# Decoder layer on one core: raw weights of the first projection set loaded a pair ahead into tiles of their own, and their decode products moved to the pair's end

## The chip, the cores and the metric

The kernel runs on one core of a Trainium2 chip. A core has an engine for matrix products (PE, with its weight loads shown apart as PEld), three engines for elementwise work (DVE, ACT, POOL) and a queue engine (SP) that here issues nearly all transfers between the chip's large memory (DRAM below) and the core's own memory. The metric is the device time of one execution in microseconds (us): the median of three runs before the change is 1027.93 us.

## The reference

One layer of a decoder, for a prompt of 2048 tokens and for 8 single tokens of a running decode with their own states. Everything is in fp32.

```
h = rmsnorm(x, norm_g)
p = h @ w_in                                   # 1024 -> 8 groups of 512
rq, rk, rv, rg, hq, hf, hi, hgate = split(p, 8)
rq, rk = rotary(rq, pos), rotary(rk, pos) * RET_DK ** -0.5
o_ret = chunked_decay_recurrence(rq, rk, rv, log_gamma, s_ret)     # 4 heads, fixed decay
o_ret = head_rmsnorm(o_ret, ret_g) * silu(rg)
logf  = logaddexp(log(lb), log1p(-lb) + log_sigmoid(hf))
kin   = (1 - lb) * sigmoid(-hf)
o_hg  = chunked_decay_recurrence(silu(hq), kin, hi, logf, s_hg)    # 4 heads, decay per channel
o_hg  = head_rmsnorm(o_hg, hg_g) * silu(hgate)
y = rmsnorm(x + concat(o_ret, o_hg) @ w_out, final_norm_g)
```

The recurrence keeps a state per head, S_t = diag(f_t) S_(t-1) + k_t v_t^T with o_t = S_t^T q_t, and is evaluated in chunks. Outputs are y for the prompt and for the decode tokens, and the new states of both.

## The kernel before, in words

**Products.** An fp32 operand is split into a high and a low part; a product is three matmuls, high x high, low x high and high x low (`three`, L350). The prompt is worked in *pairs*: 256 tokens at a time against 1024 columns of weights, both cut into 2 x 2 blocks, so that a pair takes seven block products instead of eight. A block product is 4 x 3 matmuls of 128 x 512, so a pair is 84 matmuls. The seven need sums of the weight blocks (operands T1 to T4 beside the raw B12, B22 and `wv`, which stands for B11 and B21) and sums of the token blocks (S1 to S4, made in `tok_ops`; `ab_h`, `ab_l` are the parts of the raw token blocks, L117 and L118).

**Stages.** There are three sets of eight pairs. Set 0 (pairs 0 to 7) makes the values, set 1 (pairs 8 to 15) the queries and gate of the retention, set 2 (pairs 16 to 23) its keys and the gate of the other branch, and beside set 2 the retention runs chunk by chunk (`r_steps`). Then come the projections and level products of the HGRN2 heads, and the output projection, in pairs again. Pairs 0 and 1 are done plainly, with eight block products each, while the weights arrive.

**Decode tokens.** The 8 tokens are carried through the same weights as a small extra product: `four` (L590) multiplies their 8 columns with the raw weights, 4 products of 256 columns for each 128 rows of weights. For the values this is `decode_values` (tile pvd) in pair 0; for sets 1 and 2 it is `wg_decode` (tile pgd).

**How the weights of the next set come in.** During set 0, in pairs 2 to 5, the raw weights of set 1 are brought in for k = 0 to 3: `wg_load(1, k)` loads rows k and k + 4 (tiles wgr1k, 512 KB each, L517), `wg_decode` multiplies them with the decode tokens, and `wg_spool` makes the four sums in place on DVE (`w_sums`, L503 to L506) and stores them in DRAM (ws1T1 to ws1T4, L529). In pair 7 they are fetched again. Set 2 goes the same way during set 1. The raw tiles come from a pool `rawp` with few buffers, which the token loads `xr`, the sums S and others share. The tiles of pool `vq` have one buffer for each tag (zh0, zl0, zh1, zl1, rk, rg and others), used by different things at different times.

**What sets the order.** PE's instructions keep the order in which they are written. The other engines' are ordered by a list scheduler, except that `behind(f)` ties what f issues on DVE, ACT and SP behind the last instruction issued on each. The pair loop (L908) fills a table `after`: what stands at key n is issued behind block product n (0 to 6) of the pair, and n - 0.5 is the middle of product n. Each of PE's small insertions between block products is placed in this way: the decode products, `spread` (transposes of the token statistics, tile prs, L288, from `rs_all`, which POOL makes out of `stats_sum`, ACT, L269), and `r_flip` (transposes of a chunk's keys, tile pkt, L726, whose input rk DVE makes in the rotary step at L375). The copy of prs, rb (L290), is what the scaled token blocks of the next pair need (L302), and from them come ab_h and ab_l.

**At the start.** Behind pair 0's products stand two bursts of `decode_values`, four weights in each. The sums of the value weights (`wv_comb`: `w_sums`, then the split into T1 to T4) are made in place on the raw tiles wvr0 to wvr7, so a sum waits until the decode products of its weights have read them. Before all of it stand small warm-up matmuls (L86).

**Later places.** `hgrn_rec` gives each step of a head a position within its unit, and `MOVE` shifts some of them; `levels2(1)` is a group of small products (tile plh). In the output projection the table `wd_at` places the decode steps: `d_ms` and `d_rs` normalise (DVE, tile do, L1392), `d_tr` transposes on PE (tile pdt, L1396), `wd_mm` multiplies from pair 4 on.

Of the kernel before, what the change touches and what calls it, by code (L numbers as in the profile page):

```python
# [10 lines left out]
F32 = mybir.dt.float32  # L11
# [3 lines left out]
ALU = mybir.AluOpType  # L15
# [26 lines left out]
def step_kernel(ctx, tc, a, out):  # L42
# [40 lines left out]
    for n in range(14):  # L83
        pe.matmul(wu, ones, ones, start=True, stop=True)
    for n in range(12):
        pe.matmul(wu[:32, :16], ones[:, :32], ones[:, :16], start=True, stop=True)  # L86
# [415 lines left out]
    def w_sums(r0, r1):  # L502
        dve.tensor_tensor(r0[:, 0], r0[:, 1], r0[:, 0], op=ALU.subtract)  # L503
        dve.tensor_tensor(r0[:, 1], r1[:, 1], r0[:, 1], op=ALU.subtract)
        dve.tensor_tensor(r1[:, 1], r1[:, 1], r0[:, 0], op=ALU.subtract)
        dve.tensor_tensor(r1[:, 0], r1[:, 0], r1[:, 1], op=ALU.subtract)  # L506
        return ("T2", r1[:, 1]), ("T3", r0[:, 1]), ("T1", r0[:, 0]), ("T4", r1[:, 0])

# [5 lines left out]
    def wg_load(n, k):  # L514
        for kk in (k, k + 4):
            wr[kk] = rawp.tile([P, 2, GW], F32, tag="raw", name=f"wgr{n}{kk}")
            sp.dma_start(wr[kk].rearrange("p g n -> p (g n)"), a[f"w_{n}"][kk])  # L517

    pgd = {}

    def wg_decode(n, k):
        if n not in pgd:
            pgd[n] = ps_o.tile([P, 256], F32, tag="o", name=f"pgd{n}")
        for kk in (k, k + 4):
            four(pgd[n], xs[:, kk], wr[kk].rearrange("p a b -> p (a b)"), kk == 0, kk == KT - 1)

# [60 lines left out]
    def four(ps, x, w, first, last):  # L587

        for j in range(4):
            pe.matmul(ps[32 * j : 32 * j + x.shape[1]], x, w[:, j * 256 : j * 256 + 256], start=first, stop=last)  # L590

# [203 lines left out]
    def r_steps(p):  # L795
# [112 lines left out]
    for i in range(2, n_tok):  # L908
# [267 lines left out]

    MOVE = {(0, 0, 1): 0.065, (0, 1, 3): 0.065, (0, 2, 1): 0.065, (1, 0, 1): 0.125, (1, 3, 1): 0.11}

# [693 lines left out]
    for n in range(4):  # L1872
# [108 lines left out]
```

## Time and profile before

| | |
|---|---|
| median of three runs | 1027.93 us (1026.58 to 1029.33) |
| the profiled execution | 1030.97 us, of which the span is 1029.1 us |
| granted clock of PE | 0.998 |
| PE busy | 1014.0 us, 99% of the span |
| DVE, ACT, POOL busy | 734.2, 550.3, 122.8 us |
| bytes moved | 255.63 MB, mean 248 GB/s |

The profile is one execution, and times in it count from the start of its span. A row of the timeline gives start and duration in us, the engine, the line, what is written from what, and in brackets how long the engine stood idle before it and what ended that. In a row of PE the duration is longer than the distance to the next matmul, since matmuls overlap; distances from start to start tell what a matmul costs. The view of waits sums such idle time by what was waited for. A row of windows gives, for a stretch of time, the busy time of each engine (with the number of instructions), the granted clock, the share of time in which the 16 DMA engines were busy, and the GB/s moved.

### The profile page before, as it was taken

What the parts mean: (1) busy time and instruction counts of PE and PEld (TensorE: products, weight loads), DVE (VectorE), ACT (ScalarE), POOL (GpSimd) and SP (SyncE); (2) the same over time, 40 slices, a digit from 0 to 9 for tenths busy, and PEclk for the clock granted to TensorE, in tenths of its full rate; (3) what the DMA queues carried; (4) which work ended last, traced back from release to release, by engine and by line L of the source; (5) the groups of instructions that cost most, each with busy time, mean ns of one, the idle gap of its engine ahead of it and who ended that gap; (6) DMA issues with size and microseconds to landing.
All of it is one profiled execution on the core that took longest, in us unless ns stands there. A gap on an engine that the chain in (4) does not pass through costs nothing.

```text
span 1029.1 us, 21541 instructions
## 1 busy us (share of the span) xinstructions
PE 1014.0 (99%) x8366; PEld 841.7 (82%) x8366; DVE 734.2 (71%) x1353; ACT 550.3 (53%) x1211; POOL 122.8 (12%) x231
## 2 busy tenths in 40 slices
PE   9999999999999999999999999999999999999997
PEld 7767778887778888888888899898888878878775
DVE  7887666888675885576666768768768576667886
ACT  7863435735434765555564665667556476433242
POOL 0200001000000101111111100111022112301122
PEclk9999999999999999999999999999999999999999
DMA  8699998878999965567766697555864496565652
GB/s 290 210 327 330 332 334 275 326 263 313 312 326 304 359 238 184 189 226 247 233 222 205 210 334 268 193 185 200 283 216 133 129 362 227 180 252 204 227 186 103
DMA packets 151271, 255.63 MB, mean 248 GB/s; under 512 B 11424, under 2 KB 79280, under 8 KB 151040
## 3 DMA queue, kind: packets, MB, share of 16 engines
q1 hardware_dynamic: 141408, 225.03, 64.7%
q0 software_dynamic: 7440, 24.76, 6.3%
q10 hardware_dynamic: 2320, 4.46, 1.2%
q8 instruction: 66, 1.08, 0.4%
q14 instruction: 37, 0.30, 0.1%
HBM read 166.51 MB, written 87.69 MB: 247 GB/s over the span
## 4 chain that ended last, share of the span: by engine, by line
PE 82%; DMA 4%; DVE 1%; issue 0%; SPq 0%; POOLq 0%; ACT 0%; POOL 0%; DVEq 0%; ACTq 0%
PE po L350 10%; PE pjqh L1032 9%; PE pjfh L1032 8%; PE py L1659 4%; PE plh L1246 2%; PE pur L741 1%; PE par L734 1%; PE puh L1115 1%; PE por L747 1%; PE por L749 1%; PE poh L1131 1%; DMA oT1h<-t_dramh 1%; PE poh L1133 1%; PE pv20a L350 1%; PE pv21a L350 1%; PE pv22a L350 1%
## 5 line engine op out<-in xcount | busy, mean ns | idle before, releaser
L1032 PE MATMUL pjfh<-xh,w_h 128*128 128x512 f32 (+2 forms) x160 | 59.4, 372 | 0.0
L1032 PE MATMUL pjqh<-xh,w_h 128*128 128x512 f32 (+2 forms) x160 | 58.9, 368 | 0.0
L1226 ACT ACTIVATE kepth<-kh 128x1024 f32<-128x1024 f32 x24 | 25.4, 1060 | 62.0 <-DVE kh L1216 62.0
L1032 PE MATMUL pjqh<-xh,w_l 128*128 128x512 f32 (+2 forms) x160 | 55.7, 348 | 0.0
L1032 PE MATMUL pjfh<-xh,w_l 128*128 128x512 f32 (+2 forms) x160 | 55.7, 348 | 0.0
L1032 PE MATMUL pjfh<-xl,w_h 128*128 128x512 f32 (+2 forms) x160 | 55.6, 348 | 0.0
L1032 PE MATMUL pjqh<-xl,w_h 128*128 128x512 f32 (+2 forms) x160 | 55.6, 347 | 0.0
L1216 DVE TENSOR_TENSOR kh<-kh,fph 128x512 f32<-128x512 f32 x48 | 33.4, 696 | 22.8 <-PE plh L1246 19.8
L118 DVE TENSOR_TENSOR ab_l<-xr,ab_h 128x512 fp32r<-128x512 f32 (+1 forms) x40 | 37.5, 954 | 11.6 <-ACT ab_h L117 11.6
L772 DVE SCALAR_TENSOR_TENSOR obr<-por,omr,rg 128x128 f32<-128x128 f32 x64 | 18.0, 344 | 33.3 <-POOL omr L764 28.2
L762 ACT ACTIVATE obr<-por 128x128 f32<-128x128 f32 x64 | 16.8, 277 | 44.4 <-PE por L749 40.6
L117 ACT ACTIVATE ab_h<-xr 128x512 fp32r<-128x512 f32 (+1 forms) x40 | 32.4, 838 | 11.3 <-DVE xr L302 11.3
L1032 PEld LDWEIGHTS pjqh<-xh,w_h 128*128 128x128 f32 x160 | 30.4, 190 | 4.8 <-issue 1.2
L1032 PEld LDWEIGHTS pjfh<-xh,w_h 128*128 128x128 f32 x160 | 30.2, 189 | 4.1 <-issue 0.4
L1032 PEld LDWEIGHTS pjqh<-xh,w_l 128*128 128x128 f32 x160 | 30.1, 188 | 4.1
L1032 PEld LDWEIGHTS pjfh<-xh,w_l 128*128 128x128 f32 x160 | 30.1, 188 | 4.0
L409 ACT ACTIVATE vo<-vo 128x512 f32<-128x512 f32 x32 | 20.1, 629 | 24.7 <-DVE vo L403 10.8
L1219 DVE TENSOR_TENSOR qqh<-qqh,fph 128x512 f32<-128x512 f32 x48 | 32.8, 683 | 0.0
L1032 PEld LDWEIGHTS pjqh<-xl,w_h 128*128 128x128 f32 x160 | 30.2, 189 | 3.0
L1032 PEld LDWEIGHTS pjfh<-xl,w_h 128*128 128x128 f32 x160 | 30.2, 189 | 2.7
L302 DVE SCALAR_TENSOR_TENSOR xr<-xr,g_in,rb 128x256 f32<-128x256 f32 x64 | 27.1, 480 | 7.3 <-DMA xr<-in_x_t 4.2
L1659 PE MATMUL py<-woh,oc_h 128*128 128x512 f32 x64 | 26.6, 415 | 0.0
(1839 smaller groups left out, 3335.0 us busy)
## 6 DMA issues: line engine op xcount, KB each, us to landing
xr<-a_dram SPq DMA_DIRECT2D x24, 512.0 KB
S<-s_dram SPq DMA_DIRECT2D x24, 512.0 KB
xn<-in_x_prompt SPq DMA_DIRECT2D x32, 256.0 KB
xr<-in_x_t SPq DMA_DIRECT2D x16, 512.0 KB
a_dram<-xr SPq DMA_DIRECT2D x16, 512.0 KB
s_dram<-S SPq DMA_DIRECT2D x16, 512.0 KB
wgr<-in_w SPq DMA_DIRECT2D x16, 512.0 KB
xr<-a_dram SPq DMA_DIRECT2D x32, 256.0 KB
```

Of the source, the lines that this page charges most:

```text
L117: act.activation(h, src, AF.Copy)
L118: dve.tensor_tensor(l, src, h.bitcast(F32), op=ALU.subtract)
L302: dve.scalar_tensor_tensor(r[:, k], r[:, k], g_in[:, kk : kk + 1], spread_to[i], op0=ALU.mult, op1=ALU.mult)
L350: pe.matmul(ps, xx, ww, start=(first and n == 0), stop=(last and n == 2), skip_group_check=more)
L409: act.activation(o, src, AF.Silu)
L772: dve.scalar_tensor_tensor(o[:, cc], po[:, h], ms[:, h : h + 1], rb_of[c, "g"][:, cc], op0=ALU.mult, op1=ALU.mult)
L1032: pe.matmul(ps, ww[:, kk], x[:, k, b0 : b0 + n], start=(k == 0 and i == 0), stop=(k == KT - 1 and i == 2),)
L1216: dve.tensor_tensor(kv[:, :, 0, :], kv[:, :, 0, :], two[:, :, 1:2].to_broadcast([P, nb, b]), op=ALU.mult)
L1219: dve.tensor_tensor(qv[:, :, 1, :], qv[:, :, 1, :], two[:, :, 0:1].to_broadcast([P, nb, b]), op=ALU.mult)
L1226: act.activation(ss[:, 512:], k[:, :HALF], AF.Copy)
L1246: pe.matmul(dst[32 * i : 32 * i + 32, c], kk, qq, start=True, stop=True)
L1659: pe.matmul(ps, o[:, kk], w[:, k % 4, i * 512 : (i + 1) * 512], start=(k == 0 and n == 0), stop=(k == KT - 1 and n == 2),)
```

## The change

1. `wg_load` for set 1 takes tiles of its own for six of the eight rows: for even k both rows, as two halves of 256 KB each in the tags zh0, zl0 (row k) and zh1, zl1 (row k + 4) of `vq`; for odd k row k + 4 in rk and rg, while row k stays in `rawp`. `four`, `wg_decode` and `w_sums` take such a list of two halves; the products and the four subtractions are the same.
2. The loads of set 1 are issued, tied behind what stands before them, after product 1 of pair 2 for k = 0, and after product 5 of pairs 2, 3 and 4 for k = 1, 2, 3; before, each was issued after product 0 of the pair that used it (pairs 2 to 5). Its decode products and sums follow product 6, the last of the pair; before they followed product 4 (5 in pair 3).
3. `decode_values` for all eight weights stands in one burst behind pair 0's last products; before, half of it stood behind the second quarter.
4. The statistics of the pair after next (`stats_sum`, `stats_load`) are issued after product 1 in every pair; before, after product 2 in all but pair 2.
5. In the retention's first step `r_flip(0)`, `r_score(0)` and `r_update(0)` are each issued half a product later.
6. `levels2(1)` of head 3 in the first half is issued a little earlier; `d_tr` is issued behind step 0 of pair 3 of the output projection instead of step 4 of pair 2; three more small warm-up matmuls.

```diff
@@ -84,1 +84,1 @@
-    for n in range(12):
+    for n in range(15):
@@ -502,5 +502,6 @@
     def w_sums(r0, r1):
-        dve.tensor_tensor(r0[:, 0], r0[:, 1], r0[:, 0], op=ALU.subtract)
...
+        b11, b12, b21, b22 = (r[:, g] if hasattr(r, "shape") else r[g] for r in (r0, r1) for g in range(2))
+        dve.tensor_tensor(b11, b12, b11, op=ALU.subtract)
...
     def wg_load(n, k):
-        for kk in (k, k + 4):
-            wr[kk] = rawp.tile([P, 2, GW], F32, tag="raw", name=f"wgr{n}{kk}")
-            sp.dma_start(wr[kk].rearrange("p g n -> p (g n)"), a[f"w_{n}"][kk])
+        for j, kk in enumerate((k, k + 4)):
+            if n == 1 and (j or k % 2 == 0):
+                tags = ("rk", "rg") if k % 2 else (f"zh{j}", f"zl{j}")
+                wr[kk] = [vq.tile([P, GW], F32, tag=t, name=f"wgr{n}{kk}{t}") for t in tags]
+                for g, r in enumerate(wr[kk]):
+                    sp.dma_start(r, a[f"w_{n}"][kk, :, g * GW : (g + 1) * GW])
+            else:
+                wr[kk] = rawp.tile([P, 2, GW], F32, tag="raw", name=f"wgr{n}{kk}")
+                sp.dma_start(wr[kk].rearrange("p g n -> p (g n)"), a[f"w_{n}"][kk])
...
-        if kk % 2:
-            for k in (kk - 1, kk, kk + 3, kk + 4):
+        if kk == 3:
+            for k in range(KT):
                 decode_values(k)
...
-            d = 0 if p else 0.5
+            d = 0 if p else 1
             put(3.5 + d, lambda: r_flip(ca))
-            put(4 + d if p else 6, lambda: r_load(ca, "g"))
+            put(4 if p else 6, lambda: r_load(ca, "g"))
             put(5 if 0 < p < N_V - 1 else 4.5 + d, lambda: r_score(ca), lambda: r_update(ca))
...
-            after[1 if i == 2 else 2] += [lambda i=i: behind(lambda: stats_sum(i + 2, 0)), lambda i=i: stats_load(i + 2, 1)]
+            after[1] += [lambda i=i: behind(lambda: stats_sum(i + 2, 0)), lambda i=i: stats_load(i + 2, 1)]
...
             if 2 <= j < 6:
-                after[0] += [lambda m=m, k=j - 2: wg_load(m, k)]
-                after[5 if i == 3 else 4] += [lambda m=m, k=j - 2: wg_decode(m, k), lambda m=m, k=j - 2: wg_spool(m, k)]
+                if m == 1:
+                    if j == 2:
+                        after[1] = [lambda m=m: behind(lambda: wg_load(m, 0))] + after[1]
+                    if j < 5:
+                        after[5] += [lambda m=m, k=j - 1: behind(lambda: wg_load(m, k))]
+                else:
+                    after[0] += [lambda m=m, k=j - 2: wg_load(m, k)]
+                after[6 if m == 1 else 4] += [lambda m=m, k=j - 2: wg_decode(m, k), lambda m=m, k=j - 2: wg_spool(m, k)]
...
-    MOVE = {(0, 0, 1): 0.065, (0, 1, 3): 0.065, (0, 2, 1): 0.065, (1, 0, 1): 0.125, (1, 3, 1): 0.11}
+    MOVE = {(0, 0, 1): 0.065, (0, 1, 3): 0.065, (0, 2, 1): 0.065, (1, 0, 1): 0.125, (1, 3, 1): 0.11, (0, 3, 1): -0.06}
...
-    wd_at[2] += [(0, d_ms), (2, d_rs), (4, d_tr)]
+    wd_at[2] += [(0, d_ms), (2, d_rs)]
+    wd_at[3] += [(0, d_tr)]
```

Three places show how instructions move. The first is PE's order in pair 4, where the decode products of k = 2 stand (pv4a and pv4c are banks of the pair's products, T3 and B22 weight operands, s40, s41 and ab token operands). Before:

```order
L350 MATMUL pv4a_1154<-T3l_210,s40h_1049 128x512
L590 MATMUL pgd1_922<-wgr12_1169,pk_177 8x256 x4
L590 MATMUL pgd1_922<-wgr16_1171,pk_177 8x256 x4
L350 MATMUL pv4c_1241<-B22h_213,s41h_1091 128x512
L350 MATMUL pv4c_1241<-B22l_214,s41h_1091 128x512
```

Of the change:

```order
L599 MATMUL pgd1_969<-wgr12zh0_1132,pk_180 8x256 x2
L599 MATMUL pgd1_969<-wgr12zl0_1133,pk_180 8x256 x2
L599 MATMUL pgd1_969<-wgr16zh1_1136,pk_180 8x256 x2
L599 MATMUL pgd1_969<-wgr16zl1_1137,pk_180 8x256 x2
L350 MATMUL pv5a_1354<-wv_h_208,ab_h_202 128x512
```

The same sixteen products now stand behind the last product of pair 4, ahead of the first of pair 5 (pv5a).

The loads and stores of SP about the end of pair 3 and the start of pair 4 (xr5 are the tokens of pair 5, xn the tokens for statistics, vo and v_dram results, ws1T the stored sums). Before:

```order
L344 DMA v_dram11_96<-vo3141_1112 128x512
L242 DMA xr50_1115<-in_x_t 128x1024
L242 DMA xr51_1116<-in_x_t 128x1024
L263 DMA xn00_1119<-in_x_prompt 128x512
L263 DMA xn01_1120<-in_x_prompt 128x512
L529 DMA ws1T2_128<-wgr15_990 128x512
L529 DMA ws1T3_129<-wgr11_988 128x512
L529 DMA ws1T1_127<-wgr11_988 128x512
L529 DMA ws1T4_130<-wgr15_990 128x512
L344 DMA v_dram10_95<-vo3150_1151 128x512
L517 DMA wgr12_1169<-in_w_1 128x1024
L517 DMA wgr16_1171<-in_w_1 128x1024
```

Of the change:

```order
L344 DMA v_dram11_96<-vo3141_1121 128x512
L242 DMA xr50_1124<-in_x_t 128x1024
L242 DMA xr51_1125<-in_x_t 128x1024
L263 DMA xn00_1128<-in_x_prompt 128x512
L263 DMA xn01_1129<-in_x_prompt 128x512
L521 DMA wgr12zh0_1132<-in_w_1 128x512
L521 DMA wgr12zl0_1133<-in_w_1 128x512
L521 DMA wgr16zh1_1136<-in_w_1 128x512
L521 DMA wgr16zl1_1137<-in_w_1 128x512
L344 DMA v_dram10_95<-vo3150_1152 128x512
L537 DMA ws1T2_128<-wgr15rg_951 128x512
L537 DMA ws1T3_129<-wgr11_948 128x512
```

The load of k = 2 now stands ahead of the stores of the sums of k = 1, in four pieces instead of two.

DVE at the start, from the last splits of pair 0's weights (wv_l, B12l, B22l) to the first sums of the value weights. Before, the sums stand between the splits and ahead of the token parts of pair 1 (ab_l, a21l):

```order
L118 TENSOR_TENSOR B12l1_220<-wvr2_267,B12h1_218 128x512
L503 TENSOR_TENSOR wvr0_223<-wvr0_223 128x512
L503 TENSOR_TENSOR wvr1_245<-wvr1_245 128x512
L504 TENSOR_TENSOR wvr0_223<-wvr4_228,wvr0_223 128x512
L118 TENSOR_TENSOR T1l_212<-wvr0_223,T1h_211 128x512
...
L505 TENSOR_TENSOR wvr4_228<-wvr4_228,wvr0_223 128x512
L118 TENSOR_TENSOR B22l_214<-wvr7_291,B22h_213 128x512
L506 TENSOR_TENSOR wvr4_228<-wvr4_228 128x512
L481 SCALAR_TENSOR_TENSOR ab_l_200<-x0r10_321,g_in_174,ab_h_199 128x128
```

Of the change:

```order
L118 TENSOR_TENSOR B22l_217<-wvr7_294,B22h_216 128x512
L481 SCALAR_TENSOR_TENSOR ab_l_203<-x0r10_324,g_in_177,ab_h_202 128x128
...
L481 SCALAR_TENSOR_TENSOR ab_l_203<-x0r16_330,g_in_177,ab_h_202 128x2x128
L504 TENSOR_TENSOR wvr0_226<-wvr0_226 128x512
L481 SCALAR_TENSOR_TENSOR ab_l_203<-x0r16_330,g_in_177,ab_h_202 128x2x128
L505 TENSOR_TENSOR wvr0_226<-wvr4_231,wvr0_226 128x512
L504 TENSOR_TENSOR wvr1_248<-wvr1_248 128x512
```

All sums now stand behind the token parts of pair 1.

More of the change, by code (lines that the diff above doesn't have):

```diff
@@ L502, in w_sums @@
     def w_sums(r0, r1):
[L503 to L507, printed above, removed]
+        b11, b12, b21, b22 = (r[:, g] if hasattr(r, "shape") else r[g] for r in (r0, r1) for g in range(2))
+        dve.tensor_tensor(b11, b12, b11, op=ALU.subtract)
+        dve.tensor_tensor(b12, b22, b12, op=ALU.subtract)
+        dve.tensor_tensor(b22, b22, b11, op=ALU.subtract)
+        dve.tensor_tensor(b21, b21, b22, op=ALU.subtract)
+        return ("T2", b22), ("T3", b12), ("T1", b11), ("T4", b21)
     def wv_comb(k):
@@ L524, in wg_decode @@
         for kk in (k, k + 4):
-            four(pgd[n], xs[:, kk], wr[kk].rearrange("p a b -> p (a b)"), kk == 0, kk == KT - 1)
+            halves = wr[kk] if isinstance(wr[kk], list) else [wr[kk][:, g] for g in range(2)]
+            four(pgd[n], xs[:, kk], halves, kk == 0, kk == KT - 1)
     def wg_spool(n, k):
@@ L589, in four @@
         for j in range(4):
-            pe.matmul(ps[32 * j : 32 * j + x.shape[1]], x, w[:, j * 256 : j * 256 + 256], start=first, stop=last)
+            ww = w[j // 2] if isinstance(w, list) else w[:, j // 2 * 512 : j // 2 * 512 + 512]
+            pe.matmul(
+                ps[32 * j : 32 * j + x.shape[1]], x, ww[:, j % 2 * 256 : j % 2 * 256 + 256], start=first, stop=last
+            )
     pvd = []
```

## The prediction

> **What bounds the kernel now.** I read four views in this order: the busy shares, the chain that ended last, the waits of PE, and then PE's timeline at each wait. The first two, from the page of the kernel before:
>
> ```profile
> PE 1014.0 (99%) x8366; PEld 841.7 (82%) x8366; DVE 734.2 (71%) x1353; ACT 550.3 (53%) x1211; POOL 122.8 (12%) x231
> PE 82%; DMA 4%; DVE 1%; issue 0%; SPq 0%; POOLq 0%; ACT 0%; POOL 0%; DVEq 0%; ACTq 0%
> ```
>
> PE is busy for 1014.0 of 1029.1 us and makes up 82% of the last chain. The change takes no arithmetic off it, so it can gain only where PE stands still, or where PE's stream is interrupted. The waits of PE (what waited, for what: us in total, times, longest):
>
> ```profile
> PE pgd L590 <- DMA wgr<-in_w: 2.7, 5, 0.7
> PE pkt L726 <- DVE rk L375: 1.4, 1, 1.4
> PE pdt L1396 <- DVE do L1392: 1.2, 1, 1.2
> PE wu L84 <- POOL ones L78: 1.1, 1, 1.1
> PE prs L288 <- POOL rs_all L114: 0.6, 1, 0.6
> PE pv2b L350 <- DVE ab_l L118: 0.4, 1, 0.4
> PE pv2a L350 <- ACT s L390: 0.3, 1, 0.3
> PE pv L350 <- DVE wv_l L118: 0.2, 1, 0.2
> ```
>
> The eight rows sum to 7.9 us. Four of them (pgd, pkt, pdt, prs; 5.9 us) are rows that the change moves something away from. So the gain has a ceiling near 6 us plus the cost of interrupted streams, and everything else is risk.
>
> **The decode products of set 1 (pgd).** PE's timeline around the burst in pair 4, then pair 3, pair 2 and pair 5; each row is start, duration, work, and in brackets the idle time ahead:
>
> ```profile
> 113.85 0.39 PE L350 MATMUL pv4a<-T3h,s40l 128*128 128x512 f32 x1
> 114.61 0.62 PE L590 MATMUL pgd<-wgr,pk 128*8 128x256 f32 x8 [0.37 <-DMA wgr<-in_w]
> 115.95 0.62 PE L590 MATMUL pgd<-wgr,pk 128*8 128x256 f32 x8 [0.72 <-DMA wgr<-in_w]
> 116.50 0.50 PE L350 MATMUL pv4c<-B22h,s41h 128*128 128x512 f32 x1
> ...
> 95.28 0.39 PE L350 MATMUL pv3c<-B22h,s31l 128*128 128x512 f32 x1
> 96.58 0.50 PE L350 MATMUL pv3a<-T4h,ab_h 128*128 128x512 f32 x1
> ...
> 70.80 0.39 PE L350 MATMUL pv2a<-T3h,s20l 128*128 128x512 f32 x1
> 73.35 0.50 PE L350 MATMUL pv2c<-B22h,s21h 128*128 128x512 f32 x1
> ...
> 135.69 0.39 PE L350 MATMUL pv5a<-T3h,s50l 128*128 128x512 f32 x1
> 137.88 0.50 PE L350 MATMUL pv5c<-B22h,s51h 128*128 128x512 f32 x1
> ```
>
> From the last matmul ahead of the burst to the first one behind it, pair 3 needs 96.58 - 95.28 = 1.30 us, and there nothing waits. The others need 116.50 - 113.85 = 2.65, 73.35 - 70.80 = 2.55 and 137.88 - 135.69 = 2.19. Over 1.30 that is 1.35 + 1.25 + 0.89 = **3.5 us**. In pair 4 the two waits alone are 0.37 + 0.72 = 1.09, so an interruption costs about 0.13 beside its wait; I use this below.
>
> The new code loads weight k a pair earlier for k = 1 to 3 and puts all four bursts at the pair's end. For k = 0 the load stays in pair 2:
>
> ```profile
> 62.71 1.50 SPq L517 DMA_DIRECT2D wgr<-in_w  x2
> ```
>
> Issued at 62.71, it is in full use before 73.35, so it lands 10 us after its issue at most. The change keeps its place in SP's order (early in pair 2) and asks for it two products later, at 70.80 + 0.3 + 2 x 12 x 0.227 = 76.5 (a product is 12 matmuls at 0.227). The margin is about 4 us if the issue stays where it is. The other three have about 20 us, a whole pair, instead of 8 to 9. So I take the whole 3.5 us; the bounds are 0 (all bursts still wait) and 3.5. The four half-tile DMAs in place of two put 2 more issues on SP for two of the weights and 1 more for the others, 6 in all, by the row above 0.75 us each, on a queue that PE does not follow step by step. Queued behind them are the stores of pair results and the x loads of two pairs on; what they can do is the rival on DMA below. The subtractions (L503 to L506 before) are the same four on the same engine, up to two products (5.4 us) later in each pair, and so are their spools to DRAM; the fetch is in pair 7, more than a pair after the last.
>
> **The statistics of pair 5 (prs).** They are asked for one product (2.7 us) earlier; the wait was
>
> ```profile
> 105.63 0.43 PE L288 MATMUL prs<-ident,rs_all 128*128 128x128 f32 x2 [0.58 <-POOL rs_all L114]
> ```
>
> so 0.58 + 0.13 = 0.7 goes if its loads have landed by then; bounds 0 and 0.7. I take 0.65.
>
> **The flip of the first retention chunk (pkt).** PE's timeline in pair 16 and, last, the DVE row that it waits for:
>
> ```profile
> 360.72 0.39 PE L350 MATMUL pv16a<-T3h,s150h 128*128 128x512 f32 x1
> 361.85 0.39 PE L350 MATMUL pv16a<-T3h,s150l 128*128 128x512 f32 x1
> 363.65 0.63 PE L726 MATMUL pkt<-ident,rk 128*128 128x128 f32 x4 [1.41 <-DVE rk L375]
> 364.03 0.48 PE L350 MATMUL pv16c<-B22h,s151h 128*128 128x512 f32 x1
> ...
> 362.81 0.69 DVE L375 TENSOR_TENSOR rk<-t,t 128x512 f32<-128x512 f32 x1
> ```
>
> Five matmuls pass in 361.85 - 360.72 = 1.13, so 0.226 each. The change lets six more pass ahead of the transposes, 1.36 us, against a wait of 1.41. DVE's rk is not moved by this. So 0.05 is left to wait, perhaps 0.2 with the order on DVE changed, and I take a gain of 1.4 with the interruption's 0.13 partly kept; bounds 0.9 and 1.5. The score and update of this chunk move by half a product with it, and nothing on PE's way needs them sooner.
>
> **The decode transpose (pdt).**
>
> ```profile
> 916.07 0.24 PE L1396 MATMUL pdt<-ident,do 64*128 64x64 f32 x1 [1.18 <-DVE do L1392]
> ```
>
> It moves from step 4 of pair 2 of the output projection to step 0 of pair 3, three products or 8 us later, against a wait of 1.18. Gain 1.18 + 0.07 = 1.25; the products that use it are in pairs 4 to 6, so the copy behind it has a pair's time. Bounds 1.1 and 1.3.
>
> **Small ones.** The level products of head 3 come to stand next to another group of small products (MOVE): one interruption less, 0.13 to 0.2. The three added warm-up matmuls of 32 x 16 stand ahead of a product that waits 0.2 for its weights anyway (last row of the waits): at a matmul's pace of 0.226 they would cost 0.7 less 0.2, at their size far less; I take 0, bounds 0 and 0.5.
>
> **The values' decode in one burst, and its price.** One burst of 64 takes the place of two of 32. PE at the first, and DVE around both:
>
> ```profile
> 18.55 1.91 PE L590 MATMUL pvd<-wvr,pk 128*8 128x256 f32 x32
> 20.39 0.50 PE L350 MATMUL pv<-wv_h,ab_h 128*128 128x512 f32 x1
> ...
> 19.59 1.28 DVE L503 TENSOR_TENSOR wvr<-wvr 128x512 f32<-128x512 f32 x2
> 29.24 0.68 DVE L118 TENSOR_TENSOR T3l<-wvr,T3h 128x512 fp32r<-128x512 f32 x1
> 35.14 0.69 DVE L118 TENSOR_TENSOR T2l<-wvr,T2h 128x512 fp32r<-128x512 f32 x1 [0.60 <-ACT T2h L117]
> 50.21 0.42 DVE L290 COPY rb<-prs 128x256 f32<-128x256 f32 x1 [1.34 <-PE prs L288]
> 53.86 0.69 DVE L118 TENSOR_TENSOR ab_l<-xr,ab_h 128x512 fp32r<-128x512 f32 x1 [0.72 <-ACT ab_h L117]
> 57.96 1.23 DVE L118 TENSOR_TENSOR ab_l<-xr,ab_h 128x1024 fp32r<-128x1024 f32 x1 [1.29 <-ACT ab_h L117]
> ```
>
> One interruption of the stream goes, about 0.2. But the sums of the weights overwrite what the decode products read. Before, the first started at 19.59, right behind the first burst; now none can start until the late burst has passed weight 0, near 30. Seven DVE operations that were done from 19.59 to 29.85 (two L503, one L504, T1l, L505, L506, T3l, as the order shows) come behind that time: 7 x 0.6 = 4.2 us. Of this the idle 1.34 ahead of the copy of rb takes some, and the waits for ACT within the sums (0.60 in the row above) may take more: rb comes 0.5 to 2.9 us late. Next late is ab_l for pair 2, for which PE waits 0.4 now. Ahead of it DVE idles 0.72 + 1.29 = 2.0 for ACT, which covers that much if ACT is not late too. So the loss is between 0 and 4.2 - 1.34 = 2.9; I take **0.4**, with the 0.2 gained swallowed, since PE then waits for the weights and not for its own work.
>
> **Sum.** 3.5 + 0.65 + 1.4 + 1.25 + 0.15 - 0.4 = 6.55, less 0.25 for a remaining wait at pair 2 or at pkt: **6.3 us**. The profiled execution took 1030.97 (span 1029.1), 3.0 over the median of 1027.93. 1030.97 - 6.3 = 1024.7 on its scale, and 1021.6 on that of the medians.
>
> **Rivals.**
>
> *The transfers bind.* The pairs around the loads, in 20 us windows (last two columns: share of the DMA engines, GB/s):
>
> ```profile
> 60.00:80.00 20.00, 18.67 (x92) 13.91 (x92) 17.38 (x29) 11.36 (x23) 2.13 (x3) 1.00 0.95 332
> 100.00:120.00 20.00, 18.33 (x92) 13.85 (x91) 12.98 (x23) 7.89 (x17) 1.08 (x3) 1.00 0.95 348
> 180.00:200.00 20.00, 20.00 (x91) 16.34 (x90) 17.20 (x20) 15.29 (x21) 1.09 (x2) 1.00 0.94 378
> ...
> 134.16 0.69 DVE L118 TENSOR_TENSOR ab_l<-xr,ab_h 128x512 fp32r<-128x512 f32 x1
> ```
>
> The engines are at 0.95 there, and the same bytes must pass. If an earlier load only makes another transfer later, the x rows of a later pair come late and the waits reappear under ab_l. Then only pkt, pdt and the small ones stay: 1.4 + 1.25 + 0.15 = 2.8, so **1025.1**. Against it: ab_l for pair 6 was done at 134.85, and pair 6 starts two products after 137.88, at 143.3; that is 8 us of slack, and a pair earlier is a shift in time of 4 MB, no more bytes. [...]
>
> *Slower: sums and splits take turns at the start.* If with the shortened time each of the 16 combinations goes through DVE and ACT one after the other (0.60 of waiting, 0.69 for the low part, 0.69 for the sum), they take 16 x 1.98 = 31.7 from about 30, to 61.9 instead of 48.9. That is 13 us late, less 1.34 and 2.0 of cover: 9.7 lost against the 7.0 gained elsewhere, so **1030.6**. It decides from the point where rb is copied more than 9 us later than 50.21. For it: the row with 0.60. Against it: only some of the present sums wait, and the operations on four weights may interleave.
>
> *The change does not do all that it says.* The first load is still not early: if SP's queue is held up before it by 4 us, pair 2 keeps its 1.25, and prs may keep its 0.65, while the 0.4 at the start stays: 1027.93 - 6.3 + 1.9 = **1023.5**.
>
> **How the numbers follow.** Forecast 0.60, with its own range of 1020 to 1024 (no loss at the start and no rest: 6.3 + 0.65 = 7.0 and a bit for other interruptions; loss at the start 2.9: 3.8 gained). Transfers bind 0.21, slower 0.08, only partly done 0.11. A measurement of this kernel tells 0.3%, 3.1 us, from no change: faster is below 1024.8, slower above 1031.0. Faster: 0.58 of the forecast, 0.10 of the partial case, 0.07 of the transfer case: 0.75. Slower: 0.05 of the slow case and 0.02 for a wait that I don't see: 0.07. The rest, 0.18, is no change. The range goes to 1019.5 below and to 1027.0 above, which takes in the transfer case.
>
> **What would show it.** In the waits of PE: no row for pgd, no prs, pkt at most 0.2, no pdt, the sum falling from 7.9 to about 2.5; the pgd bursts of 16 with about 1.3 from matmul to matmul, at the end of pairs 2 to 5. pvd as one burst of 64 near 30. DVE's copy of rb at 50.5 to 53, and PE's waits in pair 2 (pv2b, pv2a) at most 0.8 each. I am wrong if pgd rows stay (transfers, or SP's queue), if ab_l or prs rows appear in pairs 4 to 7 (transfers), or if pair 2 waits for more than 3 us (the start).

## The result, and the profile after

The changed kernel takes 1035.77 us (median of six runs, 1031.55 to 1037.23) against 1027.87 for the kernel before (six runs); the ratio, which is taken over all runs and not from the two medians, is 1.0068, with a 95% interval of 1.0046 to 1.009. It is slower, by more than the measurement can confuse with no change, where 6 us faster was forecast. The six runs are of two kinds: at a mean granted clock of 0.997 to 0.998 they took 1031.55 and 1033.02, at 0.993 to 0.994 1035.75 to 1037.23. The kernel before stood at 0.997 to 0.999 in each of its runs whose clock is listed.

The profiled execution is one at full clock: 1031.55 us, span 1029.8. The waits of PE in it, columns as before:

```profile
PE pv8a L350 <- ACT s L390: 2.1, 1, 2.1
PE pv8b L350 <- DVE wv_l L118: 1.5, 2, 0.8
PE wu L84 <- POOL ones L78: 1.1, 1, 1.1
PE pv8b L350 <- ACT wv_h L117: 0.9, 1, 0.9
PE pv2c L350 <- ACT p L390: 0.6, 1, 0.6
```

All four rows that were to go are gone: no pgd, prs, pkt or pdt. In their place stand the waits of pv8a and pv8b, the first products of pair 8, 4.5 us, and a new one at pv2c. PE's timeline of the changed kernel at the end of pair 4, at the flip in pair 16 and at the decode transpose shows the removed ones:

```profile
119.02 0.39 PE L350 MATMUL pv4a<-T4h,ab_l 128*128 128x512 f32 x1
...
120.31 0.50 PE L350 MATMUL pv5a<-wv_h,ab_h 128*128 128x512 f32 x1
...
366.44 0.39 PE L350 MATMUL pv16c<-B22h,s151l 128*128 128x512 f32 x1
366.67 0.60 PE L737 MATMUL pkt<-ident,rk 128*128 128x128 f32 x4
...
924.74 0.28 PE L1413 MATMUL pdt<-ident,do 64*128 64x64 f32 x1
```

The burst of pair 4 now needs 120.31 - 119.02 = 1.29 from matmul to matmul, where it needed 2.65. Where the time went is seen best from the starts of the pairs, the first matmul of each in both traces:

| from, to | before, us | after, us | difference |
|---|---|---|---|
| span's start to pair 2 | 55.51 | 55.82 | +0.31 |
| pair 2 | 23.43 | 23.48 | +0.05 |
| pair 3 | 20.51 | 20.51 | 0 |
| pair 4 | 22.64 | 20.50 | -2.14 |
| pair 5 | 21.38 | 20.51 | -0.87 |
| pairs 6 and 7 | 38.34 | 38.62 | +0.28 |
| **pair 8** | 20.10 | 25.69 | **+5.59** |
| pairs 9 to 15 | 145.47 | 145.48 | 0 |
| pair 16 | 23.99 | 22.44 | -1.55 |
| pairs 17 to 22 | 172.77 | 172.99 | +0.22 |
| pair 23 to PE's last matmul | 477.95 | 476.61 | -1.34 |

The last row ends with PE's last matmul. By pair 8 the kernel was 2.4 us ahead; pair 8 took all of that and 3.2 more. PE there:

```profile
183.26 0.50 PE L350 MATMUL pv8b<-wv_l,ab_h 128*128 128x512 f32 x1 [0.71 <-DVE wv_l L118]
185.56 0.49 PE L350 MATMUL pv8b<-wv_h,ab_h 128*128 128x512 f32 x1 [0.88 <-ACT wv_h L117]
186.82 0.50 PE L350 MATMUL pv8b<-wv_l,ab_h 128*128 128x512 f32 x1 [0.77 <-DVE wv_l L118]
190.32 0.50 PE L350 MATMUL pv8a<-T2h,s70h 128*128 128x512 f32 x1 [2.07 <-ACT s L390]
```

Pair 8 is the first of set 1. Its weight operands are fetched in pair 7 (raw B11 and B21 by SP as wg1B, the sums by POOL) and split by ACT and DVE. ACT's splits of the two halves of raw B21, first in the changed kernel, then the second half in the kernel before:

```profile
180.88 1.06 ACT L117 ACTIVATE wv_h<-wg1B 128x1024 fp32r<-128x1024 f32 x1 [5.10 <-DMA wg1B<-in_w]
184.46 1.06 ACT L117 ACTIVATE wv_h<-wg1B 128x1024 fp32r<-128x1024 f32 x1 [2.51 <-DMA wg1B<-in_w]
```

```profile
180.97 1.06 ACT L117 ACTIVATE wv_h<-wg1B 128x1024 fp32r<-128x1024 f32 x1 [2.84 <-DMA wg1B<-in_w]
```

So PE came 2.4 us earlier, and the second half landed 3.5 us later. Both rows say that ACT stood idle for a transfer, and the one of before said it too: these operands were timed by the DMA engines, not by PE, even then. Behind this split ACT has a queue of others, and behind them the copy `s` of product 0's bank, which PE needs for product 2. The copy, before and in the changed kernel:

```profile
186.20 0.58 ACT L390 ACTIVATE s<-pv8a 128x512 f32<-128x512 f32 x1
```

```profile
189.69 0.58 ACT L390 ACTIVATE s<-pv8a 128x512 f32<-128x512 f32 x1
```

It starts 5.2 us behind the split of the second half in both. Before, it ended at 186.78, and PE began product 2 at 187.25: there were 0.47 us to spare. So of the 2.4 us by which PE came earlier at most 0.47 could have been kept here, and 3.5 us of later landing make product 2 some 3.0 us later than before; it began at 190.32, 3.07 later. No run tried to put that copy ahead of the splits on ACT.

The windows of the changed kernel (last two columns: share of the DMA engines, GB/s):

```profile
160.00:165.00 5.00, 5.00 (x24) 4.14 (x23) 4.84 (x7) 2.98 (x4) 0.00 (x0) 1.00 0.57 232
165.00:170.00 5.00, 5.00 (x24) 4.14 (x23) 0.69 (x1) 2.73 (x6) 1.33 (x2) 1.00 0.99 302
170.00:175.00 5.00, 5.00 (x24) 4.14 (x23) 3.30 (x6) 3.78 (x5) 2.15 (x4) 1.00 0.99 356
175.00:180.00 5.00, 5.00 (x24) 4.14 (x23) 1.61 (x2) 0.60 (x1) 0.75 (x2) 1.00 0.99 367
180.00:185.00 5.00, 3.98 (x17) 2.63 (x15) 1.23 (x1) 1.60 (x2) 0.34 (x1) 1.00 1.04 415
185.00:190.00 5.00, 1.92 (x6) 1.05 (x6) 4.45 (x5) 5.00 (x7) 0.00 (x0) 1.00 1.04 410
```

From 165 to 190 us the engines are full (0.99 to 1.04), and the 15 us before are quiet (0.57 from 150 to 165). In the kernel before, two of these windows were not full:

```profile
165.00:170.00 5.00, 5.00 (x23) 4.13 (x23) 0.69 (x1) 3.90 (x7) 0.16 (x1) 1.00 0.87 276
170.00:175.00 5.00, 5.00 (x23) 4.13 (x22) 2.03 (x4) 1.75 (x3) 2.25 (x4) 1.00 0.73 213
```

SP's order had changed in two places. In the kernel before, it issued the halves of raw B11 at 157.5 and 164.4, and those of raw B21 at 165.7, ahead of the store of the decode gate (169.8), and at 170.5, behind it. In the changed one both halves of B11 come behind the stores of pair 7's S sums, at 164.8 and 165.5, so that 512 KB more fall into the full stretch, and both halves of B21 come behind the decode gate's store, at 171.7 and 172.1.

### The profile page after: what moved, and what is told of

The parts are those of the page before. It is cut to its first block, busy times and chain, and to the rows that moved or that the text cites. A ratio compares the mean times of both kernels' runs of the same rounds, so it can differ in the third digit from the quotient of the medians.

```text
span 1029.8 us, 21564 instructions
## 1 busy us (share of the span) xinstructions
PE 1015.2 (99%) x8372; PEld 841.7 (82%) x8372; DVE 733.8 (71%) x1353; ACT 551.5 (54%) x1211; POOL 124.5 (12%) x231
## 4 chain that ended last, share of the span: by engine, by line
PE 91%; DMA 4%; DVE 2%; ACT 1%; issue 1%; SPq 0%; POOLq 0%; POOL 0%; ACTq 0%; DVEq 0%
PE po L350 11%; PE pjqh L1049 9%; PE pjfh L1049 8%; PE py L1676 4%; PE pv L350 2%; PE plh L1263 2%; PE par L745 1%; PE puh L1132 1%; PE pur L752 1%; PE por L758 1%; PE poh L1148 1%; PE por L760 1%; DMA xn<-in_x_prompt 1%; PE poh L1150 1%; DMA wg1B<-in_w 1%; PE pv20a L350 1%
```

## The experiments

Theory A: the loss is at pair 8, because set 1's raw operands land late in a stretch in which the DMA engines are full. Rivals: ACT and DVE cannot split faster (B); the start's warm-up costs the clock (C). A second question is what lowers the clock in most runs.

**Four runs: fetch earlier; loads alone; the rest alone; fetch later in the kernel before.** The first, on the changed kernel:

```diff
-                    after[n] = [lambda m=m, op=op: wg_fetch(m, op)] + after[n]
+                    if m > 1 or n > 1:
+                        after[n] = [lambda m=m, op=op: wg_fetch(m, op)] + after[n]
+            if m == 1 and j == 6:
+                after[3] += [lambda: wg_fetch(1, "B11")]
+                after[4] += [lambda: wg_fetch(1, "B21")]
```

(so neither is fetched in pair 7).

> The changed kernel, with the raw B11 and B21 operands of set 1 (wg1B11, wg1B21) asked for in pair 6 (after its products 3 and 4) instead of in pair 7, so that SP issues them ahead of the store of the decode gate and near 162 to 164 us instead of 165 to 172. Theory A (the loss is at the start of pair 8, where the second half of wg1B21 lands at 184.4 in the changed kernel and PE stands still for 4.5 us): the waits of pv8a and pv8b shrink below 1.5 us, pair 9 starts 2 us earlier than before the change instead of 3.2 us later, and with the idle stretch gone the granted clock is back at 0.997 to 0.998 in all runs; time 1022 to 1025 us. Theory B (ACT and DVE cannot split set 1's operands faster, whenever they land): the waits at pair 8 stay above 3 us and the time stays above 1030. Theory C (the clock is lost at the start, with the three added warm-up matmuls): the waits shrink, but the clock stays at 0.993 in most runs; time 1027 to 1030.

Measured: 1037.82 us, ratio 1.0096 (1.0081 to 1.0111), clock 0.993 to 0.994 in all four runs. The waits at pair 8 were gone, and one of 8.4 us stood in pair 7. Its row, and ACT's rows ahead of it:

```profile
PE pv7c L350 <- ACT p L390: 8.4, 1, 8.4
```

```profile
172.28 0.76 ACT L544 ACTIVATE gd<-pgd 8x256 f32<-8x256 f32 x2 [2.85 <-DMA v_dram<-vo]
179.25 0.77 ACT L544 ACTIVATE gd<-pgd 8x256 f32<-8x256 f32 x2 [6.20 <-DMA v_dram<-vo]
```

The decode gate's tile gd shares three buffers with the results vo. With 2 MB of loads issued ahead of them and between them (162.4 to 166), the result stores landed late, gd waited for their buffers, and on ACT the copy of PE's bank (p) waited behind gd. The clock fell inside that wait, at 177.3 (the granted clock is 0.73 in the window from 175 to 180 us and 0.50 in the next). Late transfers were the limit here too, but putting the loads first only chose another transfer to be late. Theory C is not tested by it.

The second keeps only the loads and their decode products and puts all else back:

```diff
-    for n in range(15):
+    for n in range(12):
...
-        if kk == 3:
-            for k in range(KT):
+        if kk % 2:
+            for k in (kk - 1, kk, kk + 3, kk + 4):
...
-            d = 0 if p else 1
+            d = 0 if p else 0.5
...
-            after[1] += [lambda i=i: behind(lambda: stats_sum(i + 2, 0)), lambda i=i: stats_load(i + 2, 1)]
+            after[1 if i == 2 else 2] += [lambda i=i: behind(lambda: stats_sum(i + 2, 0)), lambda i=i: stats_load(i + 2, 1)]
...
-    wd_at[2] += [(0, d_ms), (2, d_rs)]
-    wd_at[3] += [(0, d_tr)]
+    wd_at[2] += [(0, d_ms), (2, d_rs), (4, d_tr)]
```

(the entry added to `MOVE` is taken out too).

The third keeps all else and puts the loads and their decode products back:

```diff
-            if n == 1 and (j or k % 2 == 0):
+            if False:
...
-                after[6 if m == 1 else 4] += [lambda m=m, k=j - 2: wg_decode(m, k), lambda m=m, k=j - 2: wg_spool(m, k)]
+                after[0] += [lambda m=m, k=j - 2: wg_load(m, k)]
+                after[5 if i == 3 else 4] += [lambda m=m, k=j - 2: wg_decode(m, k), lambda m=m, k=j - 2: wg_spool(m, k)]
```

> The kernel before with only the set-1 loads, their tiles and the place of their decode products changed. Theory A: the loads alone bring SP's new order (wg1B11 behind the stores of the S sums of pair 7), so pgd waits vanish (pairs 2 to 5 gain 3 us) and the start of pair 8 waits for 3 to 6 us; no gain at pkt and pdt; time 1028 to 1038, with a clock below 0.996 in some runs where the waits at pair 8 exceed 4 us. Rival (the decode burst or the statistics are to blame for pair 8): no wait above 1 us at pair 8, time 1024 to 1026.

> The changed kernel with the set-1 loads and their decode products put back as they were; burst, statistics, flip, transpose, MOVE and warm-up stay changed. SP's order at pairs 6 and 7 is that of the kernel before. Theory A: no new wait at pair 8, pgd waits stay (2.7 us), pkt and pdt waits gone (2.6 us less): time 1024 to 1026, clock 0.998. Rival: pair 8 waits for 2 us or more also here, time above 1027. Theory C (warm-up) expects a clock of 0.993 here too, time near 1030.

Loads alone: 1028.54, ratio 1.0006 (0.9994 to 1.0018). Rest alone: 1028.96, ratio 1.001 (0.9999 to 1.0021). The first two rows are waits of the loads alone, the next two of the rest alone:

```profile
PE prs L288 <- POOL rs_all L114: 1.6, 3, 0.6
...
PE pv2c L350 <- ACT p L390: 0.9, 1, 0.9
```

```profile
PE pgd L599 <- DMA wgr<-in_w: 2.2, 4, 0.6
PE plh L1257 <- issue: 1.2, 1, 1.2
```

Neither loses at pair 8, and neither gains. With the loads alone the pgd waits go, but the statistics wait in three pairs and pair 7 ends 0.05 us ahead of before: PE does not come early to pair 8. Nothing is late there either: B11 is issued as late as in the changed kernel (163.9), but the first half of B21 still goes out ahead of the decode gate's store (165.4), and the second is in use at 180.3. Theory A had expected a loss here; the loads alone make neither PE early nor B21 late. The rest alone kept the clock at 0.997 to 0.999 in ten runs with its 15 warm-up matmuls, so theory C falls. Its pkt and pdt waits were gone and the time was no better, where theory A had expected 1024 to 1026; that is taken up below.

The fourth, on the kernel before:

```diff
-                    after[n] = [lambda m=m, op=op: wg_fetch(m, op)] + after[n]
+                    at = 3 if m == 1 and op == "B21" else n
+                    if at != n:
+                        after[at] = [lambda m=m, op=op: behind(lambda: wg_fetch(m, op))] + after[at]
+                    else:
+                        after[at] = [lambda m=m, op=op: wg_fetch(m, op)] + after[at]
```

> The kernel before with one edit: raw B21 of set 1 is asked for behind product 3's place in pair 7, so that SP issues both halves behind the decode gate's store, as in the changed kernel; all else as before. Theory A: wg1B21 lands 2 to 5 us later, pair 8 waits for 2 to 5 us, and where PE stands still for most of a stretch of 8 us the granted clock falls below 0.996 in some runs; time 1030 to 1037. Rival (wg1B21 is not what sets the start of pair 8): no change, 1027 to 1029, clock 0.998.

Measured: 1028.28, ratio 1.0003 (0.9991 to 1.0015). Both halves were issued behind the decode gate's store, at 170.3, and were still in use by 177.3 and 179.2. The rival's numbers came, not theory A's. So the place behind that store is not the cause by itself: there B11 had come early (157.1 and 164.2), and POOL's fetches of the sums, which follow PE, were 2.6 us later than in the changed kernel. That what counts is how many bytes are ahead is a reading of this, not shown by it.

**Four more: gate read-out later, filler, before again, B11 early.** The first, on the changed kernel:

```diff
-                after[0] += [lambda m=m: behind(lambda: wg_decode_out(m))]
+                after[1 if m == 1 else 0] += [lambda m=m: behind(lambda: wg_decode_out(m))]
```

> The changed kernel with the read-out of set 1's decode products (gd, and SP's store of the decode gate that waits for it) one product later in pair 7, so that SP issues both halves of wg1B21 ahead of it, near 169 us instead of 171.7 to 172.1. Theory A (wg1B21 lands late because it is issued behind POOL's fetches of T1 and T3 instead of behind T2 alone): it is in use by 179 and 181 instead of 180.9 and 184.5; waits at pair 8 fall from 4.5 to under 2 us, the clock is back at 0.998, time 1024 to 1027. Rival (the DMA engines are full from 165 to 190 us whatever the order; what is put forward makes something else late): a wait of 3 us or more appears at another operand of pairs 7 or 8 (results' stores, T1, T2), time 1030 or more.

Measured: 1034.4, ratio 1.0054 (1.0035 to 1.0073), clock 0.995 to 0.996. Raw B21 was in use at 177.2 and 180.8, as theory A said, yet PE waited:

```profile
PE pv8a L350 <- DVE wv_l L118: 5.4, 1, 5.4
```

The edit also moved DVE's order: the low parts of B11, whose high parts ACT had made by 174.4, came behind those of B21 on DVE, at 183.7 to 186. The rival had expected such a wait and a time above 1030, but from a late transfer, and this one comes from DVE's order. So the run doesn't separate the theories; it does show that B21, issued 4.7 us earlier, is in use 3.6 us earlier though B11 stays in the full stretch.

The second, on the changed kernel, gives PE something to do where it stands still:

```diff
+    def pe_fill(cnt):
+        t = ps_tr.tile([P, P], F32, tag="tr", name="fill")
+        for n in range(cnt):
+            pe.matmul(t, ones, ones, start=True, stop=True)
...
+        if i == 8:
+            for key, cnt in ((0, 5), (0.5, 8), (1, 9)):
+                after.setdefault(key, []).append(lambda cnt=cnt: pe_fill(cnt))
```

> The changed kernel with 22 idle-filling products of 128x128 on ones (their result is not used) placed where PE stands still at the start of pair 8: 5 behind its product 0, 8 in the middle of product 1, 9 behind product 1, about 0.22 us each. They add no waiting for anything. If the lost clock of the changed kernel (0.993 in four of six runs, 0.998 in the profiled one) comes from PE's idle stretch at 182 to 190 us, the clock is back at 0.997 to 0.999 in every run and the median falls from 1035.8 to 1030 to 1033, though the waits for the operands stay. If the clock is lost elsewhere, it stays at 0.993 in most runs and the median at 1035 or above.

Measured: 1035.74, clock 0.996, 0.998, 0.996, 0.998. Half of the expectation held: in four runs the clock never fell to 0.993, and in the profiled one there is no half-clock stretch at pair 8 (the matmuls of pv8b that follow each other without a wait stand 0.23 to 0.24 us apart from 183.97 to 188.67; at half clock, in the last trace below, 0.43). But the median stayed. In the profiled run, at a mean clock of 0.996, PE stood still elsewhere, for no release that the profile shows:

```profile
PE puh L1140 <- issue: 2.4, 1, 2.4
```

What the two runs at 0.998 spent their time on (1035.42 and 1035.87, some 3.4 us more than the changed kernel at that clock) is not known; there is no trace of them.

The third is the kernel before, unchanged.

> The kernel before, unchanged, one more profiled execution. The one on which the prediction's sum rests took 1030.97 us, more than any of 25 later runs of this kernel (1025.7 to 1030.1). If its waits belong to the kernel, pkt (1.4), pdt (1.2), prs (0.6) and pgd (2.7) are all here again within 0.3 us. If they belong to that execution, the sum of the waits is 2 to 4 us lower here, and one or more of pkt, pdt and pgd is below half of its size.

Measured: 1031.02 us, span 1029.2. The waits of PE, and PE at the decode transpose:

```profile
PE pgd L590 <- DMA wgr<-in_w: 2.6, 5, 0.8
...
PE prs L288 <- POOL rs_all L114: 1.0, 2, 0.6
...
PE par L734 <- DMA rq<-qt_dram: 0.3, 1, 0.3
```

```profile
915.84 0.39 PE L350 MATMUL po<-woh,op2S1l 128*128 128x512 f32 x1
916.16 0.28 PE L1396 MATMUL pdt<-ident,do 64*128 64x64 f32 x1
```

pgd and prs are there again; pkt and pdt are not, at their old places. The loads alone, which leave both places as they were, have neither wait; the kernel before with the later fetch has no pkt and 0.4 of pdt; the one with the early B11, below, 0.2 of pkt. So in four further executions with unmoved places the 2.65 us that the sum took from pkt and pdt came to 0, 0, 0.4 and 0.2: they belonged to one execution. The sum of the waits is 1.7 us lower here than in the first execution, and the time is the same.

The fourth takes 1 MB out of the full stretch, on the changed kernel:

```diff
-                    after[n] = [lambda m=m, op=op: wg_fetch(m, op)] + after[n]
+                    if m > 1 or n:
+                        after[n] = [lambda m=m, op=op: wg_fetch(m, op)] + after[n]
+            if m == 1 and j == 6:
+                after[1] = [lambda: behind(lambda: wg_fetch(1, "B11"))] + after[1]
```

> The changed kernel with the raw B11 operand of set 1 (1 MB) fetched in pair 6, tied behind what stands there after product 1, near 150 us, where the DMA engines are at 0.58 in the changed kernel. SP then also has wg1B21 ahead of the decode gate's store. Theory A (too many bytes between 165 and 190): wg1B21 is in use by 178 and 180, the waits at pair 8 are under 1 us, pair 9 starts 2 us earlier than before the change; clock 0.998; time 1022 to 1026. Rival (it is the chain of ACT and DVE through set 1's operands, not their landing): the waits at pair 8 stay above 3 us.

Measured: 1026.98, ratio 0.9991 (0.9977 to 1.0005), clock 0.997 to 0.999 in ten runs. B11 was issued at 149.6 and raw B21 in use from 176.3, both halves at once:

```profile
176.33 2.00 ACT L117 ACTIVATE wv_h<-wg1B 128x1024 fp32r<-128x1024 f32 x2
```

There is no wait at pairs 7 and 8, and pair 9 starts 1.64 us earlier than before the change instead of 3.22 later. The median is 8.8 us below that of the changed kernel, 1 us above theory A's range, and can't be told from that of the kernel before. Theory A is borne out in that the late operands made the loss. B is not: the same ACT and DVE work is done in time once its operands have landed.

Why they landed late is separated only in part. This edit changed two things: SP also issued B21 at 166.7, ahead of the decode gate's store, instead of 171.7. The DMA engines are still at 1.00 to 1.04 from 170 to 190 us. With the loads alone only B11 was late, with the later fetch only B21 was issued late, and in both PE came to pair 8 at its old time; neither lost. In the changed kernel all three come together.

**Last: pair 2, and the clock.** The largest of the waits that the change had brought and that were left in that run, and ACT's rows for it:

```profile
PE pv2c L350 <- ACT p L390: 1.2, 1, 1.2
```

```profile
70.86 0.63 ACT L269 ACTIVATE xn<-xn 128x512 f32<-128x512 f32 x1 [2.38 <-DMA xn<-in_x_prompt]
...
72.44 0.57 ACT L390 ACTIVATE p<-pv2c 128x512 f32<-128x512 f32 x1
```

In the kernel before, the decode burst stood ahead of pv2c and gave ACT time to copy the bank; without it PE waits for that copy, which on ACT stands behind a square that waits for xn. One more edit on the run with B11 early:

```diff
                 stats_end(3)
+                stats_load(4, 0)
                 tok_load(3)
...
     s_split(2, 1)
-    stats_load(4, 0)
```

> The kernel with the early B11 fetch (the run before this one), with one more edit: the two loads of token statistics for pair 4 (xn40, xn41) are asked for ahead of the stores of pair 2's S sums. In the changed kernel and in that run ACT stands 2.4 us for xn41 in pair 2 and the copy of product 3's bank (p) is queued behind it, so that PE waits 0.6 to 1.25 us at pv2c. Theory: that wait falls below 0.5 us; with nothing lost at pair 8 the robust gains are the pgd waits of pairs 4 and 5 (2.2), prs (0.6) and now pair 2 (0.5 to 1), less 0.3 at the start: 2.5 to 3.5 us, time 1024 to 1026, ratio about 0.997. Rival (removed waits come back as others and the kernel keeps its median): 1027 to 1029, ratio 0.999 to 1.001.

Measured: **1024.88 us, ratio 0.9961 (0.9946 to 0.9976)** against before, 3.6 us less, at a clock of 0.998 to 0.999. It beats both kernels. In its trace pairs 2, 4 and 5 take 1.52, 2.14 and 0.88 us less than in the table's column before, and pair 8 takes 20.12 us. The waits that are left:

```profile
PE wu L84 <- POOL ones L78: 1.1, 1, 1.1
PE pv2a L350 <- ACT s L390: 0.3, 1, 0.3
PE pv2b L350 <- DVE ab_l L118: 0.2, 1, 0.2
PE plh L1266 <- issue: 0.2, 1, 0.2
```

The early B11 in the kernel before, as a control (the same diff):

> The kernel before with only the early fetch of B11 (in pair 6, after product 1). If the early fetch alone makes the kernel faster, the time is 1026 to 1027 here too, as with the change; if it only mends what the change breaks, the kernel keeps its time: 1027.5 to 1028.5, with pgd waits of 2.3 to 2.7 and nothing at pair 8.

Measured: 1026.98, ratio 0.9993 (0.998 to 1.0005), with 3.8 us of waits at pgd. The median lies where the early fetch alone was to put it if it made the kernel faster, but the interval holds no change, so this run can't tell whether it gains something there. What is clear is that with the early fetch the kernel before and the changed one are alike (0.9993 and 0.9991), while without it the changed one is slower. The earlier statistics loads were not tried in the kernel before.

And the changed kernel twice more, for a trace at the lower clock:

> The changed kernel, unchanged, one more profiled execution. The first one had a clock of 0.998 and 1031.55 us, four of the other five 0.993 to 0.994 and 1035.8 to 1037.2. [...]

> The changed kernel, unchanged, a third profiled execution, to have its own trace at the lower clock: the first two profiled ones stood at 0.998 and 0.999 (1031.55 and 1032.18 us), four timed ones at 0.993 to 0.994 (1035.8 to 1037.2). [...]

The first took 1032.18 at 0.999, with the same waits at pair 8 and no stretch at half clock there (1.00 in every window from 160 to 210 us). The second took 1035.62 at 0.993. Its windows at pair 8 (the third number from the end is the granted clock):

```profile
180.00:184.00 4.00, 3.08 (x14) 2.22 (x12) 0.25 (x1) 1.06 (x1) 0.55 (x1) 1.00 1.04 416
184.00:188.00 4.00, 2.48 (x7) 1.15 (x6) 1.64 (x2) 1.76 (x2) 0.00 (x0) 0.77 1.03 409
188.00:192.00 4.00, 2.65 (x6) 1.49 (x5) 4.00 (x5) 4.00 (x7) 0.00 (x0) 0.50 1.00 377
192.00:196.00 4.00, 3.89 (x9) 3.15 (x10) 4.00 (x5) 3.83 (x5) 0.00 (x0) 0.50 0.89 288
196.00:200.00 4.00, 4.00 (x18) 3.27 (x18) 3.97 (x6) 0.68 (x2) 0.00 (x0) 0.95 0.59 201
```

By these windows the clock is halved from 186.2 to 196.4, for 10.24 us (1.84 us of the one with 0.77, all 8 of the two with 0.50, 0.4 of the one with 0.95), in the middle of the waits; pair 9 starts at 208.91 instead of 205.13. Ten microseconds at half speed cost, by estimate, some 5, less what PE would have waited anyway; measured are 3.4 us between these two executions (1035.62 - 1032.18). That is the size of the difference between the two kinds of runs; the four other runs at 0.993 to 0.994 have no trace.

## Why the prediction was wrong

1. **The path after set 0 was costed at nothing: this is the step that failed.** The prediction followed the spools to "the fetch is in pair 7, more than a pair after the last" and stopped there. It asked whether the sums were stored in time, and neither what PE meets at pair 8 when it comes earlier nor what the moved issues do to SP's order there. Of the removed waits some 5.9 us did go in the profiled execution (pairs 4, 5, 16 and from 23 on), and pair 8 cost 5.59 at full clock. The second half of raw B21, for which ACT already idled 2.84 us before, left 0.47 us to spare; PE came 2.4 us earlier and this half 3.5 us later. That the DMA engines were nearly full there was in view: the window at 180 to 200 stood in the prediction with 0.94, and nothing about pair 8 was drawn from it. The rival "the transfers bind" had the mechanism, an earlier load that makes another transfer late, but looked for it at the token rows of pairs 4 to 7 and priced it as a gain lost, not as a loss. None of the signs of being wrong that the prediction named came.
2. **The clock was left out.** No term or rival had it. In five of eight executions of the changed kernel the mean clock is 0.993 to 0.994, and in the one of these that has a trace it is halved for 10 us in the waits of pair 8. That moved the median from about 1032 to 1035.8.
3. **pgd, 3.5 us:** right for pairs 4 and 5 (with prs, 2.0 + 0.89 predicted, 2.14 + 0.87 measured), wrong for pair 2. There 1.25 was taken as gained, and pair 2 is no shorter: the wait had covered a copy on ACT, for which PE now stands 0.62 at pv2c, and smaller delays within the pair's first and last products took the rest. The step "So I take the whole 3.5 us" looked at the load that was waited for and not at who is late next.
4. **pkt and pdt, 1.4 + 1.25:** right in size against the profiled execution (1.55 in pair 16, 1.34 from pair 23 on), but that is luck, for these waits were no costs of the kernel. Pair 16 takes 22.72 to 22.80 us in the four further executions with the flip at its old place and 22.44 in every one with it moved, so the move is worth 0.3. The stretch from pair 23 on took 477.9 us in the second execution of the kernel before too, without a wait at pdt, and 476.5 with the loads alone, the transpose at its old place. The step that fails is the scale: waits that were read in an execution "3.0 over the median" were taken off the median too, as if they were in it. In the second execution they were absent and the time was as high.
5. **The start, -0.4:** measured -0.31, but this can't be told from chance: pair 2 starts at 55.51 and 55.93 in the two executions of the kernel before and at 55.00 to 55.94 in the three of the changed one. The rival that the sums take turns did not come. The warm-up matmuls cost nothing that shows.
6. **The range** (to 1027.0) and the chance of 0.07 for slower were too narrow for a change that moves PE and SP's order ahead of a stretch that had not been read.

What stays open: which of the two changes in SP's order, with PE's earlier arrival, makes raw B21 late; why both profiled executions of the kernel before took some 3 us more than its median; and the time of the two filler runs at full clock.

## What to carry to other kernels

When PE is made earlier, follow it to the next stage and look for an engine that already idles for a transfer there: that operand did not come sooner here (ACT idled 2.84 us for raw B21 before, and it was in use 3.5 us later), and the gain ended at it. When loads are moved on a queue, list what the queue issues in the next stage too, before and after. In a stretch where the DMA engines are full, putting one transfer ahead can make another late (the 8.4 us here, with the engines at 1.04 from 170 to 180 us); look for a quiet stretch (here 150 to 165 us, at 0.57) and move bytes into it. Before a wait of about a microsecond is counted as a gain, see it in a second execution.

## What the runs showed of the hardware

In the changed kernel's trace at 0.993 the clock was halved although PE had not idled for long at a time: before the fall at 186.2 us stand two gaps, of 0.92 and 0.76 us. In its two traces at 0.998 and 0.999 the waits at pair 8 are no shorter (4.5 and 4.6 us in all, the longest 2.1, against 3.9 and 1.0 here), and the granted clock stays at 1.00, in the one from 165 to 190 us and in the other from 160 to 210. So much the same waits came with a halved clock in one execution and with a full one in two others; what decides it was not shown.

Two more traces have the fall inside one long wait of PE. With the earlier fetch PE stood still from 174.2 to 182.7 us, and the granted clock is 0.73 from 175 to 180, 0.50 from 180 to 185 and 0.74 from 185 to 190: some 10.3 us at half clock, from 177.3 on. With the gate read-out later PE stood still from 179.6 to 184.9, and 0.72 from 180 to 185 and 0.60 from 185 to 190 make some 6.8 us, from 182.2 on. In both the clock was still halved when PE took up work again: its matmuls stood 0.43 us apart until 187.5 and 188.9, and 0.23 behind that.

A load of 512 KB was not in use until 9 to 12 us after its issue when the engines stood at 0.99 to 1.04 (raw B21: issued at 171.7 to 172.1, used at 180.9 and 184.5), and stores issued behind such loads kept their buffers long enough for an 8.4 us wait on PE in the run with the earlier fetch.
